# Block 1's out and down products with tokens on the partitions, seven products for eight in two pairs of k-tiles

## The chip, the cores and the metric

The kernel runs on one core of one Trainium2 chip. The metric is the device time of one execution in microseconds. Before the change the median of 3 runs is 2539.73 us (2539.48 to 2539.82). One further execution was recorded by the hardware profiler; all durations below come from it.

## The reference

Two transformer blocks on 256 tokens of width 2048, in fp32. The change lies in the end of the first block (`w_out` is 2048 x 2048, `w_gate` and `w_up` are 2048 x 5632, `w_down` is 5632 x 2048):

```python
    h = h + mixed @ w_out                                        # "out"
    hn = rmsnorm(h, ffn_norm)
    h = h + (silu(hn @ w_gate) * (hn @ w_up)) @ w_down           # "gu", then "down"
return rmsnorm(h, final_norm)                                    # input of block 2
```

Block 2 begins with another rmsnorm and a large input projection, of which the values `dv` are taken first.

## The kernel before, in words

Precision. TensorE multiplies in a rounded fp32 format, so every operand is split into a high and a low part and a product takes three matmuls: high by high, high by low, low by high. Weights arrive from HBM in pieces `raw` of 128 x 1024 (512 KB, one DMA on SyncE's queue, 6 buffers). ScalarE copies a piece into `wh`, VectorE subtracts into `wl` (`halves`, L391 to L398). `wh` and `wl` have 4 buffers each, and a fifth from the pool `wx1` while out, gu and down run. So a piece can be split only when TensorE has finished the piece four or five places earlier. Activations are split the same way by `hl` (L418 to L422). A k-tile is 128 rows of a weight.

Two forms of a product. In the form of `mm_w` (L434, L435) the weight is the stationary operand and all 256 tokens stream: a matmul of 512 columns (high weight by both halves of the input) and one of 256 columns. The result has output columns on the partitions, its two halves are added by `sum_halves` (L572 on ScalarE, L575 on VectorE). Out (L434, 8 groups of 2 output tiles) and down are done so. In the form of `group_t` (L525) 128 tokens are stationary and 512 weight columns stream: three matmuls of 512 columns per product, tokens on the partitions. gu is done so: 11 groups, each with 512 columns of gate and 512 of up, 16 pieces (one k-tile each), 4 products per piece. The result goes through Silu (L1030) and a multiply (L1031) to the tile `z`, and TensorE turns it back by 8 transposes per group (L1042), which `hl` splits for down.

Order. Part p of the FFN is 4, 4 and 3 groups of gu, then down over those 16, 16 and 12 k-tiles, added to h (L1068). In the last part each finished tile of h is split for block 2 (`hl` with `gfp`), squared twice on ScalarE (`sq`, 2 buffers) and the squares are summed on GpSimd (`ssq`, L605); the two norms follow (L613, L623). The program is written as Python in program order with small tasks (`pump`, `tick`) set between matmuls; the framework below it places the instructions of each engine in one list, and an engine works through its list in order. `group_t` has code for pairs of k-tiles, which `PAIRS = 0` switches off.

Of the kernel before, what the change touches and what calls it, by code (L numbers as in the profile page):

```python
# [28 lines left out]
PARTS_T = ((0, 16), (16, 16), (32, 12))  # L29
UCOLS = 2048  # L30
PAIRS = 0
# [18 lines left out]
def weight_plan():  # L50
# [50 lines left out]
    for g in range(8):  # L101
        group(("out", g), "w_out", range(16), [(256 * g, 256 * g + 256)])
    for p, (i0, n) in enumerate(PARTS_T):
        for g in range(i0 // 4, (i0 + n) // 4):
            cr = [(512 * g, 512 * g + 512)]
            for c in range(PAIRS // 2):
                ka, kb = [2 * c, 2 * c + 1], [PAIRS + 2 * c, PAIRS + 2 * c + 1]
                unit(("gup", g, c, 0), ("w_gate", ka, cr), ("w_up", kb, cr))
                unit(("gup", g, c, 1), ("w_up", ka, cr), ("w_gate", kb, cr))
            for k in range(2 * PAIRS, KD, 2):  # L110
                unit(("guk", g, k), ("w_gate", [k], cr), ("w_up", [k], cr), ("w_gate", [k + 1], cr), ("w_up", [k + 1], cr))
        chunks = _chunks(range(i0, i0 + n))
        for g, c in [(0, 0), (1, 0), (0, 1), (1, 1)] + [(g, c) for g in range(2, 8) for c in range(2)]:
            unit(("down", p, g, c), ("w_down", chunks[c], [(256 * g, 256 * g + 256)]))
# [24 lines left out]
def _width(ranges):  # L139
# [10 lines left out]
FIRST_OPS = ("B11", "t3", "t1", "B22", "B21", "t2", "t4")  # L150
OPS2 = (("B11", 0), ("B11", 1), ("t3", 0), ("t3", 1), ("t1", 0), ("t1", 1), ("B22", 0), ("B21", 0),
        ("t2", 0), ("t2", 1), ("B22", 1), ("B21", 1), ("t4", 0), ("t4", 1))
assert PAIRS in (0, 4)


def stream():

    out, u = [], 0
    while u < len(PLAN):
        key, n = PLAN[u][0], UNIT_COLS[u]  # L160
        if key[0] == "lat":
# [81 lines left out]

class Prog:
# [5 lines left out]
    def __init__(self, tc, t, dbg=None, stop=None):  # L250
# [7 lines left out]
        self.look, self.far, self.held = 2, 4, {}  # L258
# [75 lines left out]
    def take(self):  # L334

        self.fill(1)
        return self.split.pop(0)

    def fill(self, n=None):
        while len(self.split) < (n or self.look):  # L340
            if not self.raws and not self.fetch():
                return
            while len(self.raws) <= self.far and self.fetch():
                pass
            self.divide()

# [3 lines left out]
    def fetch(self):  # L350
# [3 lines left out]
        nc, w = self.nc, self.t["w"]  # L354
        p = STREAM[self.nraw]
        self.nraw += 1
        if len(p) == 3:
            u, a, b = p
            raw = self.raw(b - a)
            nc.sync.dma_start(raw[:, :b - a], w[u][:, a:b])  # L360
        else:
            op, u = p
            if op == "B11":
                raw = self.wx.tile([P, 1024], F32, tag="sum", name="sum", bufs=4)
                nc.sync.dma_start(raw, w[u][:, 0:1024])
                self.held[u] = raw
            elif op in ("t1", "t2", "t4"):
                raw = self.held[u]
            else:
                raw = self.raw(1024)  # L370
                v, a = {"B22": (u, 1024), "B21": (u + 1, 1024), "t3": (u + 1, 0)}[op]
                nc.sync.dma_start(raw, w[v][:, a:a + 1024])
                if op == "t3":
                    nc.gpsimd.dma_start(raw, w[u][:, 1024:2048], accum_op=ALU.add)
# [3 lines left out]
    def divide(self):  # L378

        nc, w = self.nc, self.t["w"]  # L380
        p, raw = self.raws.pop(0)
        n = p[2] - p[1] if len(p) == 3 else 1024
        self.split.append((p, *self.halves(raw, n)))
        if len(p) == 2:
            u = p[1]
            add = {"B11": (u + 1, 0), "t1": (u, 1024), "t2": (u + 1, 1024)}.get(p[0])
            if add:
                nc.gpsimd.dma_start(raw, w[add[0]][:, add[1]:add[1] + 1024], accum_op=ALU.add)

    def halves(self, raw, n):  # L390
        nc = self.nc  # L391
# [4 lines left out]
        nc.scalar.activation(wh[:, :n], raw[:, :n], AF.Copy)  # L396
        nc.vector.tensor_tensor(wl[:, :n], raw[:, :n], wh[:, :n].bitcast(F32), op=ALU.subtract)  # L397
# [66 lines left out]

# [28 lines left out]
    def combos(self, xa, xb):  # L493
# [5 lines left out]
        nc.vector.tensor_tensor(f[:, 0, :], a2, b2, op=ALU.subtract)  # L499
        nc.vector.tensor_tensor(f[:, 1, :], a1, f[:, 0, :], op=ALU.subtract)  # L500
        nc.vector.tensor_tensor(f[:, 2, :], b1, f[:, 1, :], op=ALU.subtract)
        nc.vector.tensor_tensor(f[:, 3, :], a1, a2, op=ALU.subtract)
        o = self.ffp.tile([P, 2, 4, P], F32R, tag="combo", name="combo", bufs=PAIRS)
# [4 lines left out]
    def group_t(self, xs, cs, before_std=None):  # L508
# [4 lines left out]
        self.one = 7  # L513
        nstd = KD - 2 * PAIRS
        banks = [self.psp.tile([P, 512], F32, tag=f"bank{i}", name="q", bufs=1) for i in range(7)]
        std = [[0, 1], [2, 3]] if not PAIRS else [[1, 2], [3, 7]]
        left = [3 * PAIRS] * 7 + [0]
        for r in std:
            for i in r:
                left[i] += 3 * nstd  # L520
        begun = [False] * 8

        def mm(i, x, w):
            left[i] -= 1
            nc.tensor.matmul(banks[i], x, w, start=not begun[i], stop=left[i] == 0)  # L525
            begun[i] = True
            self.tick(229)

        def product(i, x, w):
            mm(i, x[0], w[0])  # L530
            mm(i, x[0], w[1])
            mm(i, x[1], w[0])
# [3 lines left out]
        for _ in range(7 * (PAIRS // 2)):  # L536
            (op, u), wh, wl = self.take()
            self.fill()
            c = PLAN[u][0][2]
            for i in range(2):  # L540
                a = 2 * c + i
                b = a + PAIRS
                w = [h[:, 512 * i:512 * i + 512] for h in (wh, wl)]
# [1005 lines left out]
```

## Time and profile before

| what | value |
|---|---|
| median of 3 runs | 2539.73 us |
| profiled execution, its own time | 2539.54 us |
| its span in the profile | 2537.7 us |
| TensorE busy | 2507.2 us, 99% of the span |
| VectorE busy | 1633.6 us, 64% |
| ScalarE busy | 1313.2 us, 52% |
| GpSimd busy | 129.7 us, 5% |
| out | 523 to 612 us |
| gu and down, part 1 | 612 to 792, 792 to 883 us |
| gu and down, part 2 | 883 to 1061, 1061 to 1152 us |
| gu and down, part 3 | 1152 to 1286, 1286 to 1354 us |
| first group of dv (block 2) | 1354 us to about 1370 us |

The time lies 1.8 us above the span: what is before the first and after the last recorded instruction. Matmuls are pipelined, so the rows of a busy TensorE overlap; what one costs is the distance between two starts.

### The profile page before, as it was taken

What the parts mean: (1) busy time and instruction counts of PE and PEld (TensorE: products, weight loads), DVE (VectorE), ACT (ScalarE), POOL (GpSimd) and SP (SyncE); (2) the same over time, 40 slices, a digit from 0 to 9 for tenths busy, and PEclk for the clock granted to TensorE, in tenths of its full rate; (3) what the DMA queues carried; (4) which work ended last, traced back from release to release, by engine and by line L of the source; (5) the groups of instructions that cost most, each with busy time, mean ns of one, the idle gap of its engine ahead of it and who ended that gap; (6) DMA issues with size and microseconds to landing.
All of it is one profiled execution on the core that took longest, in us unless ns stands there. A gap on an engine that the chain in (4) does not pass through costs nothing.

```text
span 2537.7 us, 35945 instructions
## 1 busy us (share of the span) xinstructions
PE 2507.2 (99%) x13756; PEld 2168.1 (85%) x13756; DVE 1633.6 (64%) x2379; ACT 1313.2 (52%) x1983; POOL 129.7 (5%) x149
## 2 busy tenths in 40 slices
PE   9999999999999999999999999999999999999997
PEld 8988888888888888888889888888888888888886
DVE  8866775876455544555467677666876567656765
ACT  6565565554444444444456555555655455545553
POOL 3000000001000000000022000003100000000002
PEclk9999999999999999999999999999999999999998
DMA  6544555565555555555555544454555555555552
GB/s 235 201 156 142 172 176 187 188 214 202 184 187 187 189 189 187 189 185 190 187 174 179 193 156 153 143 202 153 171 186 183 191 191 187 182 192 188 190 175 92
DMA packets 131725, 458.52 MB, mean 181 GB/s; under 512 B 14624, under 2 KB 17056, under 8 KB 131296
## 3 DMA queue, kind: packets, MB, share of 16 engines
q1 hardware_dynamic: 130608, 452.78, 52.9%
q10 hardware_dynamic: 944, 3.43, 0.4%
q8 instruction: 108, 1.77, 0.3%
q14 instruction: 65, 0.53, 0.1%
HBM read 454.06 MB, written 2.10 MB: 180 GB/s over the span
## 4 chain that ended last, share of the span: by engine, by line
PE 96%; DVE 3%; ACT 1%; issue 0%; DMA 0%; POOL 0%; POOLq 0%; SPq 0%; ACTq 0%; DVEq 0%
PE acc L434 42%; PE acc L435 21%; PE q L525 19%; PE acc L432 3%; PE acc L480 2%; PE acc L479 2%; PE acc L481 2%; PE acc L431 2%; PE ms L685 1%; PE ms L1209 1%; DVE hl L422 1%; PE ms L714 1%; PE tr L1042 0%; DVE wl L397 0%; PE acc L1340 0%
## 5 line engine op out<-in xcount | busy, mean ns | idle before, releaser
L434 PE MATMUL acc<-hl,wh 128*128 128x512 f32 x4642 | 1646.0, 397 | 7.7 <-DVE hl L422 6.3
L397 DVE TENSOR_TENSOR wl<-raw,wh 128x1024 fp32r<-128x1024 f32 (+4 forms) x882 | 1052.5, 1196 | 704.5 <-ACT wh L396 700.6
L396 ACT ACTIVATE wh<-raw 128x1024 fp32r<-128x1024 f32 (+4 forms) x882 | 907.3, 1031 | 774.9 <-PE acc L434 428.7
L435 PE MATMUL acc<-hl,wl 128*128 128x256 f32 x4642 | 1300.0, 281 | 0.6 <-DVE wl L397 0.5
L434 PEld LDWEIGHTS acc<-hl,wh 128*128 128x128 f32 x4642 | 872.1, 188 | 207.9 <-DVE hl L422 5.7
L435 PEld LDWEIGHTS acc<-hl,wl 128*128 128x128 f32 x4642 | 876.5, 189 | 10.4 <-DVE wl L397 1.9
L525 PE MATMUL q<-wh,hl 128*128 128x512 f32 x1408 | 438.8, 392 | 0.4 <-ACT z L1030 0.4
L525 PEld LDWEIGHTS q<-wh,hl 128*128 128x128 f32 x1408 | 263.0, 188 | 56.2 <-ACT z L1030 0.9
L525 PE MATMUL q<-wl,hl 128*128 128x512 f32 x704 | 275.6, 392 | 0.0
L572 ACT ACTIVATE ev<-acc 128x256 f32<-128x256 f32 x352 | 129.3, 384 | 216.8 <-PE acc L432 215.3
L605 POOL TENSOR_TENSOR ssq<-ssq,sq 128x256 f32<-128x256 f32 x92 | 87.6, 961 | 2058.7 <-ACT sq L595 1585.3
L575 DVE TENSOR_TENSOR tmp<-acc,ev 128x256 f32<-128x256 f32 x321 | 126.5, 422 | 76.5 <-ACT ev L572 76.3
L525 PEld LDWEIGHTS q<-wl,hl 128*128 128x128 f32 x704 | 132.3, 188 | 28.7
L432 PE MATMUL acc<-hl,wh 128*128 128x512 f32 x352 | 132.0, 395 | 0.0
L431 PE MATMUL acc<-hl,wl 128*128 128x256 f32 x352 | 100.8, 286 | 0.0
L480 PE MATMUL acc<-wl,hl 128*128 128x512 f32 (+4 forms) x264 | 90.6, 343 | 2.4 <-DVE wl L397 2.4
L479 PE MATMUL acc<-wh,hl 128*128 128x512 f32 (+4 forms) x264 | 92.4, 350 | 0.0
L481 PE MATMUL acc<-wh,hl 128*128 128x512 f32 (+4 forms) x264 | 90.4, 343 | 0.0
L431 PEld LDWEIGHTS acc<-hl,wl 128*128 128x128 f32 x352 | 66.1, 188 | 8.3 <-issue 0.3
L432 PEld LDWEIGHTS acc<-hl,wh 128*128 128x128 f32 x352 | 66.4, 189 | 7.5
L480 PEld LDWEIGHTS acc<-wl,hl 128*128 128x128 f32 x264 | 49.8, 189 | 5.8 <-DVE wl L397 3.0
L481 PEld LDWEIGHTS acc<-wh,hl 128*128 128x128 f32 x264 | 49.7, 188 | 3.0
(243 smaller groups left out, 1238.9 us busy)
## 6 DMA issues: line engine op xcount, KB each, us to landing
raw<-in_w_dram SPq DMA_DIRECT2D x801, 512.0 KB, 3.6
raw<-in_w_dram SPq DMA_DIRECT2D x18, 384.0 KB, 3.2
raw<-in_w_dram SPq DMA_DIRECT2D x16, 362.0 KB, 4.1
raw<-in_w_dram SPq DMA_DIRECT2D x16, 346.0 KB, 3.6
raw<-in_w_dram SPq DMA_DIRECT2D x15, 256.0 KB, 3.2
raw<-in_w_dram SPq DMA_DIRECT2D x8, 364.0 KB, 3.7
raw<-in_w_dram SPq DMA_DIRECT2D x8, 348.0 KB, 3.6
x<-in_xT_dram SPq DMA_DIRECT2D x8, 256.0 KB, 5.7
```

What stands on the lines that cost most here:

```text
L396: nc.scalar.activation(wh[:, :n], raw[:, :n], AF.Copy)
L397: nc.vector.tensor_tensor(wl[:, :n], raw[:, :n], wh[:, :n].bitcast(F32), op=ALU.subtract)
L431: nc.tensor.matmul(acc[:, S:], wl, x[:, 0, :], start=False, stop=False)
L432: nc.tensor.matmul(acc, wh, x, start=False, stop=True)
L434: nc.tensor.matmul(acc, wh, x, start=first, stop=False)
L435: nc.tensor.matmul(acc[:, S:], wl, x[:, 0, :], start=False, stop=last)
L479: nc.tensor.matmul(acc, xh, wh, start=(k == 0), stop=False)
L480: nc.tensor.matmul(acc, xh, wl, start=False, stop=False)
L481: nc.tensor.matmul(acc, xl, wh, start=False, stop=(k == n - 1))
L525: nc.tensor.matmul(banks[i], x, w, start=not begun[i], stop=left[i] == 0)
L572: nc.scalar.activation(e, acc[:, S:], AF.Copy)
L575: nc.vector.tensor_tensor(out, acc[:, :S], e, op=ALU.add)
```

## The change

Out and down now use the form of `group_t`: 2 groups of 1024 output columns each, for out over 16 k-tiles, for down over 16, 16 and 12. h lies with tokens on the partitions (`h0`, `h1`, loaded from a second copy of x, `xtok`), and what the next stage needs is turned by `turned`: after out 32 transposes, after the last down 32.

In every group of out, gu and down four k-tiles form two pairs. For a pair the 2 x 2 block product (two halves of the tokens, two k-tiles, two blocks of 512 columns) is computed by seven products (`OPS`) in place of eight, after Winograd. The activation side of it, four differences per pair, is made once by `combos`. The weight side, four sums per pair (`t1`, `t3`, `t2`, `t4`), is made anew in every group by VectorE, in place in the raw pieces (L431, 128 x 1024 for both pairs at a time), and each sum is split like a piece. So the four pieces of the two pairs give seven pieces for TensorE (6 matmuls each) and the other k-tiles give one each (12 matmuls). Four of the seven results are combined at the end of the pair part (`sums`, "early", L616 to L620), four accumulators hold the rest until the end of the group ("late", L1156 in gu, L636 in out and down). In out and down both are added to h (L632, L636).

Banks, look-ahead and raw buffers are kept by hand (`map`, `look`, `ahead`, `live`); the pool `wx1` is gone, so `wh` and `wl` have four buffers. Tiles of h for block 2 are turned two at a time (`done`): per tile `hl`, two squares with their GpSimd sums, and a copy of h. The transposes of the second half stand in the first group of `dv`.

```diff
+OUT_PAIRS = ((0, 1), (2, 3))
+GU_PAIRS = ((0, 4), (1, 5))
+DOWN_PAIRS = ((0, 1), (2, 3))
...
-PAIRS = 0
...
+    def tgroup(key, w, kts, pairs, col):
+        kts = list(kts)
+        w1, w2 = (w, w) if isinstance(w, str) else w
+        c1 = [(col, col + 512)]
+        c2 = [(col + 512, col + 1024)] if isinstance(w, str) else c1
+        for c in range(0, len(pairs), 2):
+            pp = pairs[c:c + 2]
+            ka, kb = [kts[a] for a, _ in pp], [kts[b] for _, b in pp]
+            seg = lambda w, kk, c: [(w, [k], c) for k in kk]
+            unit(key + ("pair", c, 0), *seg(w1, ka, c1), *seg(w2, kb, c2))
+            unit(key + ("pair", c, 1), *seg(w2, ka, c2), *seg(w1, kb, c1))
+        rest = [k for i, k in enumerate(kts) if not any(i in p for p in pairs)]
+        for i in range(0, len(rest), 2):
+            unit(key + ("std", i), *[x for k in rest[i:i + 2] for x in ((w1, [k], c1), (w2, [k], c2))])
...
-    for g in range(8):
-        group(("out", g), "w_out", range(16), [(256 * g, 256 * g + 256)])
+    for g in range(2):
+        tgroup(("out", g), "w_out", range(16), OUT_PAIRS, 1024 * g)
...
-            unit(("down", p, g, c), ("w_down", chunks[c], [(256 * g, 256 * g + 256)]))
+            tgroup(("gu", g), ("w_gate", "w_up"), range(16), GU_PAIRS, 512 * g)
+        for g in range(2):
+            tgroup(("down", p, g), "w_down", range(i0, i0 + n), DOWN_PAIRS, 1024 * g)
...
+OPS = ("B11", "B22", "t1", "t3", "t2", "B21", "t4")
+ROLES = {"B11": 0, "B22": 1, "t1": 2, "t3": 3, "t2": 4, "B21": 5, "t4": 6, "std": 7}
+EARLY, LATE = (0, 2, 3, 4), (1, 5, 6, 7)
...
+            if op == "t1":
+                parts["B12"] = get(u + 1, 0, n)
+            elif op in ("B11", "B22"):
+                parts[op] = get(u, 0 if op == "B11" else n, n if op == "B11" else 2 * n)
+            elif op == "B21":
+                parts[op] = get(u + 1, n, 2 * n)
...
+            to, a, b = {"B11": ("B11", 0, 0), "B22": ("B22", 0, 0), "B21": ("B21", 0, 0), "t1": ("B11", "B11", "B12"),
+                        "t3": ("B12", "B12", "B22"), "t2": ("B11", "B11", "B22"), "t4": ("B11", "B11", "B21")}[op]
+            raw = parts[to]
+            if op == "t2":
+                self.live -= 1
+            if a:
+                self.nc.vector.tensor_tensor(raw[:, :n], parts[a][:, :n], parts[b][:, :n], op=ALU.add)
...
+        def product(r, x, w):
+            if r not in b:
+                b[r] = place(r)
+            for i, j in ((0, 0), (0, 1), (1, 0)):
+                nc.tensor.matmul(b[r], x[i], w[j], start=left[r] == total[r], stop=left[r] == 1)
+                left[r] -= 1
+                self.tick(229)
...
+            for op in OPS:
+                p, wh, wl = self.take()
+                self.fill()
+                for i, (ka, kb) in enumerate(pairs[c:c + 2]):
+                    w = [h[:, 512 * i:512 * i + 512] for h in (wh, wl)]
+                    cmb = lambda m: (cs[c + i][:, 0, m, :], cs[c + i][:, 1, m, :])
+                    x = {"B11": lambda: cut(xs[ka], t0), "B21": lambda: cut(xs[kb], t0), "B22": lambda: cmb(2),
+                         "t4": lambda: cut(xs[kb], t1), "t1": lambda: cmb(0), "t2": lambda: cmb(1),
+                         "t3": lambda: cmb(3)}[op]()
+                    product(op, x, w)
...
+        if pairs:
+            early(b)
...
+        late(b)
+        self.map = [self.map[i] for i in EARLY + LATE]
+        self.one = self.map[7]
...
+    def sums(self, b):
+        e, v, w, c = [self.fz.tile([P, 512], F32, tag="ft", name="ft", bufs=4) for _ in range(4)]
+        nc.scalar.activation(e, b["B11"], AF.Copy)
+        nc.vector.tensor_tensor(v, b["t2"], e, op=ALU.subtract)
+        nc.vector.tensor_tensor(w, b["t1"], v, op=ALU.add)
+        nc.vector.scalar_tensor_tensor(c, b["t3"], -1.0, w, op0=ALU.mult, op1=ALU.add)
+        nc.vector.tensor_tensor(v, b["t3"], v, op=ALU.subtract)
+        return e, w, v, c
+    LATE_OF = ("B21", "B22", "t4", "std")
+    def residual(self, h, g):
+        at = [h[t][:, 1024 * g + 512 * m:1024 * g + 512 * m + 512] for t in range(2) for m in range(2)]
+        def early(b):
+            for a, x in zip(at, self.sums(b)):
+                nc.vector.tensor_tensor(a, a, x, op=ALU.add)
+        def late(b):
+            for a, r in zip(at, self.LATE_OF):
+                nc.vector.tensor_tensor(a, b[r], a, op=ALU.add)
...
+    def turned(self, src, n, done, wait):
+        for i in range(0, n, 2):
+            b = self.bank("tr")
+            for j in range(2):
+                for t in range(2):
+                    o = 256 * j + 128 * t
+                    self.nc.tensor.transpose(b[:, o:o + P], src[t][:, (i + j) * P:(i + j + 1) * P], self.cst("ident"))
+            for j in range(2):
+                done(i + j, b[:, 256 * j:256 * j + 256])
+            yield
...
+            for a, b in OUT_PAIRS:
+                if j == b:
+                    cm.append(self.combos(gates[a][0], za, self.cbp))
...
+            early, late = self.residual(h, g)
+            self.group_t(("out", g), mixed, cm, OUT_PAIRS, early, late)
...
+                def late(b):
+                    for i, r in enumerate(self.LATE_OF):
+                        if sb_:
+                            nc.vector.tensor_tensor(sb_[i], b[r], sb_[i], op=ALU.add)
+                        else:
+                            sb_.append(b[r])
+                self.group_t(("gu", g), hn, cs, GU_PAIRS, early, late)
...
+                early, late = self.residual(h, g)
+                operands = Acts(acts, n)
+                self.group_t(("down", p, g), operands, ca, DOWN_PAIRS, early, late,
+                             lambda k: k >= need and self.finish(t0))
+                if last:
+                    src = [h[t][:, 1024 * g:1024 * g + 1024] for t in range(2)]
+                    def done(i, s, g=g):
+                        nonlocal sa, sb
+                        j = 8 * g + i
+                        x2.append(self.hl(s, self.gfp[:, j:j + 1]))
+                        sa = self.stat_add(sa, s)
+                        sb = self.stat_add(sb, s, self.col("final_norm", j))
+                        r = self.resp.tile([P, S], F32, tag="res", name="res", bufs=16)
+                        nc.scalar.activation(r, s, AF.Copy)
+                        hs.append(r)
+                    t0 = self.add(self.turned(src, 8, done, 3), urgent=True)
...
+            accs = self.group_a(lambda c: (c == 2 and self.finish(tx), self.load("dv", g, c))[1], x, 4, n)
...
-                self.wx = c2.enter_context(tc.tile_pool(name="wx1", bufs=1))
-                self.wxn = 1
```

On VectorE, at the seam from one gu group to the next, this stands in the list before (wl: the split of a piece, L397; z: the multiply with up; hl: the split of a turned tile):

```order
L397 TENSOR_TENSOR wl<-raw,wh 128x1024 x14
L1031 SCALAR_TENSOR_TENSOR z<-q,small,z 128x512 x2
L397 TENSOR_TENSOR wl<-raw,wh 128x1024
L419 TENSOR_TENSOR hl<-tr,hl 128x256 x2
L397 TENSOR_TENSOR wl<-raw,wh 128x1024
L419 TENSOR_TENSOR hl<-tr,hl 128x256 x2
```

A group has 16 splits of pieces, two multiplies and four small splits, and no sum of weights. At the same seam the list is now (L453: split; L431: sum of two raw pieces; L1156: late sum; L1129: z; L479: hl; L617: first of the early sums):

```order
L431 TENSOR_TENSOR raw<-raw 128x1024 x2
L453 TENSOR_TENSOR wl<-raw,wh 128x1024
L1156 TENSOR_TENSOR ft<-q,ft 128x512
L453 TENSOR_TENSOR wl<-raw,wh 128x1024
L1156 TENSOR_TENSOR ft<-q,ft 128x512 x3
L1129 SCALAR_TENSOR_TENSOR z<-ft,small,z 128x512 x2
L431 TENSOR_TENSOR raw<-raw 128x1024
L453 TENSOR_TENSOR wl<-raw,wh 128x1024 x3
L431 TENSOR_TENSOR raw<-raw 128x1024
L479 TENSOR_TENSOR hl<-tr,hl 128x256
L617 TENSOR_TENSOR ft<-q,ft 128x512
L453 TENSOR_TENSOR wl<-raw,wh 128x1024
```

In front of the first row stands the split of B11; the splits after it are B22, t1, then t3, t2, B21, and last t4. Four sums of 1024 columns, four late sums and the two multiplies have come between the seven splits.

On ScalarE, at the entry to block 2, the list before (hl: high part of an input tile of block 2; sq: a square, which waits for GpSimd to free one of its two buffers; wh: a piece's high part; ev: half of an accumulator):

```order
L396 ACTIVATE wh<-raw 128x692 x2
L572 ACTIVATE ev<-acc 128x256 x2
L396 ACTIVATE wh<-raw 128x692
L421 ACTIVATE hl<-res,gfp 128x256
L595 ACTIVATE sq<-res 128x256
L595 ACTIVATE sq<-res,cc 128x256
L421 ACTIVATE hl<-res,gfp 128x256
L595 ACTIVATE sq<-res 128x256
L595 ACTIVATE sq<-res,cc 128x256
L396 ACTIVATE wh<-raw 128x692 x2
```

Two tiles are left to be squared there when dv begins. Now the eight rows behind the first of the following stand there four times, for the eight tiles of the second half, each time after the transposes of two tiles:

```order
L449 ACTIVATE wh<-raw 128x692
L481 ACTIVATE hl<-tr,gfp 128x256
L680 ACTIVATE sq<-tr 128x256
L680 ACTIVATE sq<-tr,cc 128x256
L1181 ACTIVATE res<-tr 128x256
L481 ACTIVATE hl<-tr,gfp 128x256
L680 ACTIVATE sq<-tr 128x256
L680 ACTIVATE sq<-tr,cc 128x256
L1181 ACTIVATE res<-tr 128x256
```

The second `hl` of a block stands behind the first tile's squares and copy, and all four pairs of tiles go through one bank of PSUM.

## Rows read from the trace of the kernel before

**Rows 1.** The page's chain that ended last, shares of the span by engine.
```profile
PE 96%; DVE 3%; ACT 1%; issue 0%; DMA 0%; POOL 0%; POOLq 0%; SPq 0%; ACTq 0%; DVEq 0%
```

**Rows 2.** Stretches, busy PE PEld DVE ACT POOL us (instructions), clock, DMA share, GB/s.
```profile
523.00:612.00 89.00, 89.00 (x510) 77.68 (x509) 62.57 (x79) 49.03 (x77) 11.65 (x13) 1.00 0.64 219
657.00:792.00 135.00, 134.65 (x599) 109.90 (x600) 67.52 (x67) 59.33 (x68) 0.00 (x0) 1.00 0.55 187
792.00:883.00 91.00, 91.00 (x524) 79.66 (x524) 51.86 (x68) 40.41 (x53) 0.00 (x0) 1.00 0.55 186
1286.00:1354.00 68.00, 68.00 (x391) 59.35 (x390) 50.99 (x72) 44.86 (x84) 23.71 (x27) 1.00 0.48 161
1354.00:1372.00 18.00, 18.00 (x119) 17.79 (x119) 13.97 (x31) 11.58 (x22) 4.64 (x6) 1.00 0.54 179
```

**Rows 3.** TensorE in order of time, end of out: start us, us, instruction.
```profile
610.00 0.39 PE L434 MATMUL acc<-hl,wh 128*128 128x512 f32 x1
610.24 0.28 PE L435 MATMUL acc<-hl,wl 128*128 128x256 f32 x1
610.35 0.39 PE L434 MATMUL acc<-hl,wh 128*128 128x512 f32 x1
```

**Rows 4.** TensorE in order of time, in gu.
```profile
745.46 0.39 PE L525 MATMUL q<-wl,hl 128*128 128x512 f32 x1
...
746.14 0.39 PE L525 MATMUL q<-wl,hl 128*128 128x512 f32 x1
```

**Rows 5.** TensorE in order of time, four transposes between the matmuls of gu.
```profile
661.60 0.61 PE L1042 MATMUL tr<-cc,z 128*128 128x128 f32 x4
661.97 0.47 PE L525 MATMUL q<-wl,hl 128*128 128x512 f32 x1
662.29 0.63 PE L525 MATMUL q<-wh,hl 128*128 128x512 f32 x2
```

**Rows 6.** VectorE in order of time in gu; in brackets the idle time before and its releaser.
```profile
1239.42 1.23 DVE L397 TENSOR_TENSOR wl<-raw,wh 128x1024 fp32r<-128x1024 f32 x1 [1.49 <-ACT wh L396]
1240.56 1.40 DVE L1031 SCALAR_TENSOR_TENSOR z<-q,small,z 128x512 f32<-128x512 f32 x2
```

**Rows 7.** Groups on VectorE and ScalarE: busy us, mean ns of one, idle before, releaser.
```profile
L397 DVE TENSOR_TENSOR wl<-raw,wh 128x1024 fp32r<-128x1024 f32 x801 | 981.0, 1227 | 668.2 <-ACT wh L396 664.7 <-PE acc L1340 2.0
L575 DVE TENSOR_TENSOR tmp<-acc,ev 128x256 f32<-128x256 f32 x321 | 126.5, 422 | 76.5 <-ACT ev L572 76.3
L419 DVE TENSOR_TENSOR hl<-tr,hl 128x256 fp32r<-128x256 f32 x44 | 18.4, 421 | 10.9 <-ACT hl L418 10.9
L1031 DVE SCALAR_TENSOR_TENSOR z<-q,small,z 128x512 f32<-128x512 f32 x22 | 15.5, 744 | 1.0 <-ACT z L1030 0.8 <-issue 0.2
L396 ACT ACTIVATE wh<-raw 128x1024 fp32r<-128x1024 f32 x801 | 845.5, 1057 | 717.2 <-PE acc L434 397.4 <-PE q L525 251.7 <-issue 29.9
```

**Rows 8.** Waits on ScalarE, 657 to 792 us: total, times, longest.
```profile
ACT wh L396 <- PE q L525: 66.4, 43, 1.8
```

**Rows 9.** GpSimd in order of time, at the entry to block 2.
```profile
1356.97 3.25 POOL L605 TENSOR_TENSOR ssq<-ssq,sq 128x256 f32<-128x256 f32 x4 [3.45 <-ACT sq L595]
1363.75 0.70 POOL L623 TENSOR_TENSOR small<-small,mhalf 128x2 f32<-128x2 f32 x1 [3.52 <-DVE small L628]
```

**Rows 10.** Stretches around two stalls of TensorE in block 2, as rows 2.
```profile
1764.50:1766.70 2.20, 0.00 (x0) 0.00 (x1) 2.20 (x4) 1.55 (x5) 1.99 (x3) 0.98 0.65 257
1766.70:1769.90 3.20, 3.17 (x10) 2.72 (x11) 3.20 (x4) 1.02 (x2) 3.20 (x5) 0.50 0.00 0
1773.30:1776.20 2.90, 0.42 (x3) 0.10 (x1) 2.90 (x5) 1.88 (x5) 2.90 (x4) 1.00 0.00 0
1776.20:1780.10 3.90, 3.88 (x14) 3.23 (x15) 3.90 (x8) 2.79 (x7) 2.15 (x3) 0.58 0.00 0
```

**Rows 11.** Waits on TensorE over the whole span, gu's: total, times, longest.
```profile
PE q L525 <- ACT z L1030: 0.4, 1, 0.4
```

**Rows 12.** The page's DMA issues: KB each, median us from issue to landing.
```profile
raw<-in_w_dram SPq DMA_DIRECT2D x801, 512.0 KB, 3.6
```

More of the change, by code (lines that the diff above doesn't have):

```diff
@@ L378, in divide, with low_due, high @@
     def divide(self):
-        nc, w = self.nc, self.t["w"]
         p, raw = self.raws.pop(0)
[L382 to L391, printed above, removed]
+        if isinstance(p[0], int):
+            n = p[2] - p[1]
+        else:
+            op, u, n = p
+            parts = self.parts[u]
+            to, a, b = {"B11": ("B11", 0, 0), "B22": ("B22", 0, 0), "B21": ("B21", 0, 0), "t1": ("B11", "B11", "B12"),
[5 more added lines that the diff above has]
+                self.nc.vector.tensor_tensor(raw[:, :n], parts[a][:, :n], parts[b][:, :n], op=ALU.add)
+        wh, wl = self.high(raw, n)
+        self.low_due()
+        self.due = (wl, raw, wh, n, p[0])
+        self.split.append((p, wh, wl))
+    def low_due(self):
+        if self.due:
+            self.low(*self.due[:4])
+            if self.due[4] not in ("B11", "t1", "t2", "B22"):
+                self.live -= 1
+            self.due = None
+    def high(self, raw, n):
         self.nhalf += 1
@@ L506, in combos, with group_t @@
         return o
-    def group_t(self, xs, cs, before_std=None):
+    def group_t(self, key, xs, cs, pairs, early, late, extra=None):
         nc = self.nc
[L513 to L532, printed above, removed]
+        n = len(xs)
+        paired = {k for p in pairs for k in p}
+        rest = [k for k in range(n) if k not in paired]
+        b = {}
+        place = lambda r: self.psp.tile([P, 512], F32, tag=f"bank{self.map[ROLES[r]]}", name="q", bufs=1)
+        self.one = self.map[7]
+        left = dict.fromkeys(OPS, 3 * len(pairs))
+        std = (("B21", "B22"), ("t4", "std"))
+        left["std"] = 0
+        for r in std[0] + std[1]:
+            left[r] += 3 * len(rest)
+        total = dict(left)
+        def product(r, x, w):
[5 more added lines that the diff above has]
+                self.tick(229)
@@ L534, in group_t @@
         t0, t1 = slice(0, P), slice(P, S)
         cut = lambda x, ts: (x[:, 0, ts], x[:, 1, ts])
[L536 to L543, printed above, removed]
-                cmb = lambda n: (cs[a][:, 0, n, :], cs[a][:, 1, n, :])
-                q, x = {"B11": (0, cut(xs[a], t0)), "B21": (1, cut(xs[b], t0)), "B22": (2, cmb(2)),
-                        "t4": (3, cut(xs[b], t1)), "t1": (4, cmb(0)), "t2": (5, cmb(1)), "t3": (6, cmb(3))}[op]
-                product(q, x, w)
@@ L1073, in block1_ffn @@
+        self.look, self.ahead = 2, False
+        self.fill()
+        self.one, self.trb = None, (self.nbank + 7) % 8
         n1, n12 = Norm(), Norm()
         def factors():
+            while not t0.done:
+                yield
             yield
```

297 lines of the change are left out of this document (139 added, 158 removed).

## The prediction

> **What bounds the kernel now.** I read the chain of waits first: 96% of it is TensorE, and DMA has nothing [rows 1]. [...] Three gu groups take 135.0 us, so one takes 45.0. Then the distances between matmul starts, since busy rows overlap. In the form of out and down one k-tile by 128 output columns takes 0.35 us (610.00 to 610.35) [rows 3]; two of them do the work of one product of gu, which takes 0.68 us (745.46 to 746.14), 0.227 per matmul [rows 4]. Last, what VectorE and ScalarE wait for: the split of a weight piece waits for its high part, and that waits for TensorE to free a buffer [rows 6, 7, 8]. So the splitters run on a leash of four or five pieces. On the average they have time to spare, but they cannot work ahead of the leash.
>
> The sum is made against the profiled execution, 2539.5 us, which lies 0.2 us under the median of the runs.
>
> **What TensorE saves.** Seven for eight: 2 pairs in each of 2 + 11 + 6 = 19 groups, 38 products by 0.68 = 25.8 us less. The other form: out and down are 16 x 8 + 44 x 8 = 480 products, each 2 x 0.35 - 0.68 = 0.02 us cheaper, 9.6 us less. Against it stand 64 more transposes. Four of them and one matmul take 661.60 to 662.29, 0.69 us [rows 5]; without the matmul's 0.227 that is 0.115 each, 7.4 us more. Alone, these would make 28.0 us less. That the products are really gone is not in doubt: the lists show the seven names and no eighth.
>
> The halves of the accumulators that ScalarE and VectorE added in out and down go (each 0.42 us on VectorE) [rows 7]. Neither engine is on the chain there, so I give nothing for it.
>
> **What the pair part costs.** TensorE's side first, with its zero where it starts on B11: six matmuls per piece, so 1.36 us each; it wants B22 at 1.36, t1 at 2.72, t3 at 4.08, t2 at 5.44, B21 at 6.8, t4 at 8.16, and the first ordinary piece at 9.53. An ordinary piece lasts 2.72. With four buffers a split can begin when the piece four places earlier is done: B11 at -8.16, B22 at -5.44, t1 at -2.72, t3 at 0.
>
> VectorE's side. A split takes 1.23 us, but the next instruction starts after 1.14 (1239.42 to 1240.56) [rows 6]. No row shows a sum of two 1024-column fp32 pieces; the split is the same operation on the same shape, so I take 1.14 for it too; bounds are 0.42 (the row of a quarter of the size) and 1.23 [rows 7]. For a late sum or the first early sum (512 columns, from PSUM) no row stands either; between 0.42 (half the size) and 0.74 (the z multiply) I take 0.61: the row of half the size and 0.28 more (a quarter of the split's 1.14 for a quarter of its columns), less the 0.09 by which the next one starts early. By the same 0.09 or so a multiply z is 0.66 and a small split 0.34 [rows 7]. From the first split of the pair part to the first ordinary one, a gu group that follows a gu group gives VectorE 8 splits and 4 sums (13.7 us), 4 late sums (2.4), 2 multiplies (1.3), 2 small splits (0.7), one early sum (0.6): 18.7 us. It can begin at -6.85 (-8.16, the drain of the last matmul, 1.06 for the high part [rows 7]) and would end at 11.9 without a pause. TensorE wants that last split at 9.75, or 10.55 with its eight transposes counted in, which I do above and in the old 45.0 us.
>
> In the order of the list: B11 to -5.7; two sums to -3.4; split of B22 to -2.3; a pause for the first late sum, whose accumulator TensorE ends at -1.9, to -1.2; split of t1 to -0.1; three late sums, each after its last matmul, to 1.75; two multiplies to 3.1; sum t2 to 4.2; split of t3 to 5.35, wanted at 4.3. The high part of t2 follows its sum, to 5.4, and TensorE's list has a matmul with it ahead of the rest of t3, so TensorE pauses about 0.8 there. Splits of t2 and B21 to 7.7; sum t4 to 8.9; its high part, ScalarE, to 10.1, while VectorE does a small split and the early sum; split of t4 to 11.2; small split; first ordinary split to 12.7. TensorE has paused for t4 from 9.3 to 10.1 and from 10.3 to 11.4, and gets the first ordinary piece going at about 13.2 with the transposes done. That is 2.6 us late. Behind it the ordinary pieces need 2.72 us of TensorE and 1.14 of VectorE each, and VectorE is back at its leash within three of them.
>
> This holds for 8 gu groups and for the 3 first halves of down (which follow a gu group). The other 8 pair parts (both of out, the gu groups behind out or down, the second halves of down) have no multiplies and mostly no small splits before t4: the same count gives t4's split at 9.9 to 10.4 and 1.7 to 2.2 us late, more in the second half of out, where small splits stand ahead of t4; I take 2.1. Sum: 11 x 2.6 + 8 x 2.1 = 45.4 us. Bounds: below, the queue without any pause, 11 x 1.3 + 0 = 14; above, with full durations (20 instructions by 0.09 more), 11 x 4.3 + 8 x 3.7 = 77.
>
> **The entry to block 2.** Before, two tiles were left when dv began, and TensorE stood still nowhere in 1354 to 1372 [rows 2]. Now eight tiles are turned there through one bank, two at a time. ScalarE may square only when GpSimd has freed a buffer, and GpSimd takes 0.81 us per sum (four in 3.25) [rows 9], so 1.6 per tile. With the high part, the copy and a weight piece in between a round of two tiles takes 3.3 to 4.1 us. In it TensorE has 12 dv matmuls of 346 columns (346/512 of 0.227 = 0.153 each), its transposes and in two rounds six matmuls of the next group: 2.3 to 3.2 us. Four rounds lose 4 to 6 us, and the norm behind them (matmul, 0.70 on GpSimd [rows 9], matmul) loses about 2, since GpSimd's last sums end later than the tiles. I take 7; bounds 0 (all hidden by moving matmuls forward) and 13.
>
> **The sum.** 2539.5 - 25.8 - 9.6 + 7.4 + 45.4 + 7 = 2563.9 us, in a measurement 2564. With the bounds of the unknown prices 2526 (14 and 0) to 2602 (77 and 13).
>
> **Rivals.** A: the pair parts are hidden. Against it stands the queue above; for it, that VectorE is idle 30 to 50% of these stages [rows 2] and that pauses between groups were 0.4 us at most [rows 11]. With 0.4 per pair part, 7.6 us, and the entry at 7, the time is 2526, with a free entry 2519. The change gains as long as a pair part loses less than (28.0 - 7)/19 = 1.1 us.
>
> [...]
>
> C, slow too: raw pieces late. The sums are made in place, so the raw buffer of B11 is free only after t4's split at 11.2; the piece loaded into it lands 3.6 us later [rows 12], is split by 17.5 and wanted at 18.6. If landings take 5 us when four are issued together, each group loses about 1 us more, 19 us, 2583.
>
> D: no overlap between VectorE's instructions, and 77 us for the pair parts: 2539.5 - 28.0 + 77 + 7 = 2595. The rows speak against it (1.14 from start to start, 1.23 of duration) [rows 6]. [...]
>
> **Chances and range.** Forecast (pair parts of 1.3 to 4 us) 0.55, A 0.25, B 0.10, C 0.06, D 0.04. The forecast's own range is 2545 to 2585. The range for 8 in 10 takes A in down to 2518 and B, D up to 2596. What a measurement of this kernel tells from no change is about 0.2%, 5 us: faster (under 2534.7) holds A and nothing else, 0.25; within it a little of A and of the forecast's low end, 0.08; slower 0.67.
>
> **What would show it.** In the changed kernel's profile TensorE should wait in every pair part, for the split or the high part of t3, t2 and t4 (L453, L449), 2 to 3 us in a gu group, and a gu group should take 45.5 to 46.5 us, where A has 43.5. Out should take 88 to 91 us, down of 16 k-tiles 89 to 92. VectorE should show no idle time from -6 to 13 us around a pair part. At the entry TensorE should wait for ScalarE's hl behind GpSimd's sums. I am wrong if the waits at t4 are under 1 us, if VectorE's sums turn out much shorter than a split, or if the granted clock falls in gu.

## The result and the profile after

The changed kernel takes 2558.91 us (median of 4 runs, 2558.57 to 2559.29) against 2539.78 of the kernel before in the same session: 1.0076 times as long, 95% interval 1.0058 to 1.0093. The forecast was 2564, slower, range 2518 to 2596. The profiled span is 2557.5 us; 19.8 us were added.

The chain of waits that ended last in the changed kernel, from its page, stands against [rows 1]: VectorE now has a tenth of it, and the weight sums (L431) and splits (L453) stand on it by name.

```profile
PE 85%; DVE 10%; issue 2%; ACT 2%; DMA 0%; POOL 0%; POOLq 0%; ACTq 0%; SPq 0%; DVEq 0%
PE acc L494 33%; PE q L578 23%; PE acc L495 17%; DVE wl L453 4%; PE acc L492 2%; PE acc L527 2%; PE acc L526 2%; PE acc L528 1%; DVE raw L431 1%; PE acc L491 1%; ACT wh L449 1%; PE ms L770 1%; DVE ft L1156 1%; DVE hl L482 1%; PE ms L1326 1%
```

The changed kernel by stage, columns as in [rows 2]: out, four gu groups, a down of 16 k-tiles, the next four gu groups, the last three, and the entry to block 2 with its dv products.

```profile
522.30:612.40 90.10, 88.07 (x389) 71.00 (x388) 75.27 (x93) 49.88 (x66) 0.00 (x0) 1.00 0.61 210
612.40:794.30 181.90, 177.22 (x786) 143.22 (x785) 142.59 (x166) 97.19 (x120) 0.69 (x1) 1.00 0.56 185
794.30:884.60 90.30, 87.45 (x381) 70.26 (x380) 71.14 (x77) 42.21 (x45) 0.00 (x0) 1.00 0.55 187
884.60:1065.20 180.60, 175.18 (x770) 141.71 (x769) 138.82 (x154) 91.04 (x105) 0.00 (x0) 1.00 0.55 187
1155.50:1290.40 134.90, 130.76 (x575) 106.17 (x574) 104.25 (x116) 68.41 (x79) 0.00 (x0) 1.00 0.56 187
1361.80:1423.20 61.40, 55.06 (x324) 50.58 (x324) 34.99 (x64) 34.86 (x67) 14.40 (x20) 0.97 0.48 164
```

The eleven gu groups take 181.9 + 180.6 + 134.9 = 497.4 us, 45.2 each on the mean. In the kernel before, three of them took 45.0 each [rows 2] and all eleven 44.8 on the mean (from the first gu product to the first of down: 611.74 to 792.29, 882.64 to 1061.51 and 1152.10 to 1285.97 us). TensorE has 1.36 us less to do in a group (two products by 0.68) and yet needs longer. VectorE is busy 78% of the time in gu. The clock is 1.00 in all lines but the last.

Where the 19.8 us lie is read from the starts of the first dv product and of the first product behind that stage, in the lists of TensorE in order of time. Kernel before:

```profile
1354.42 0.33 PE L479 MATMUL acc<-wh,hl 128*128 128x346 f32 x1
1402.22 0.39 PE L434 MATMUL acc<-hl,wh 128*128 128x512 f32 x1
```

Changed kernel:

```profile
1361.86 0.32 PE L526 MATMUL acc<-wh,hl 128*128 128x346 f32 x1
1423.19 0.39 PE L494 MATMUL acc<-hl,wh 128*128 128x512 f32 x1
```

So 7.4 us are lost until dv begins, 13.5 in the dv stage (61.3 for 47.8), and 1.1 come back later; why stays open.

Now one pair part, that of a gu group that follows a gu group, VectorE in order of time (start, duration, what ended the idle time before it; "..." stands for rows left out). TensorE's zero is the start of its first product of B11, 1.37 before its first product with a combination of activations, which starts at 750.06: 748.69.

```profile
741.84 1.23 DVE L453 TENSOR_TENSOR wl<-raw,wh 128x1024 fp32r<-128x1024 f32 x1 [1.49 <-ACT wh L449]
743.10 2.49 DVE L431 TENSOR_TENSOR raw<-raw 128x1024 f32<-128x1024 f32 x2
...
747.47 1.22 DVE L453 TENSOR_TENSOR wl<-raw,wh 128x1024 fp32r<-128x1024 f32 x1
...
750.40 1.41 DVE L1129 SCALAR_TENSOR_TENSOR z<-ft,small,z 128x512 f32<-128x512 f32 x2
751.72 1.22 DVE L431 TENSOR_TENSOR raw<-raw 128x1024 f32<-128x1024 f32 x1
752.86 3.57 DVE L453 TENSOR_TENSOR wl<-raw,wh 128x1024 fp32r<-128x1024 f32 x3
756.34 1.22 DVE L431 TENSOR_TENSOR raw<-raw 128x1024 f32<-128x1024 f32 x1
...
758.68 1.22 DVE L453 TENSOR_TENSOR wl<-raw,wh 128x1024 fp32r<-128x1024 f32 x1 [0.19 <-ACT wh L449]
```

A sum takes 1.22 and the next instruction starts 1.14 later (751.72 to 752.86), as the prediction took it. In this pair part the queue runs to a tenth of a microsecond as it was counted: B11's split from -6.85, t1's done at 0.0, the multiplies at 3.1, t3's, t2's and B21's splits at 7.7, t4's sum at 8.9, t4's split at 11.2. TensorE in the same stretch:

```profile
753.04 0.60 PE L649 MATMUL tr<-cc,z 128*128 128x128 f32 x4
754.09 0.50 PE L578 MATMUL q<-wh,combo 128*128 128x512 f32 x1 [0.44 <-ACT wh L449]
...
757.87 0.39 PE L578 MATMUL q<-wh,hl 128*128 128x512 f32 x1
758.70 0.50 PE L578 MATMUL q<-wh,hl 128*128 128x512 f32 x1 [0.44 <-ACT wh L449]
759.92 0.50 PE L578 MATMUL q<-wh,hl 128*128 128x512 f32 x1 [0.72 <-ACT wh L449]
```

From start to start it loses 0.6 in front of t2's product (1.05 for four transposes, which need 0.46), 0.6 in front of t4's (0.83 for 0.227) and 1.0 behind its first matmul (1.22 for 0.227); with 0.3 for the matmuls that start slowly after a stop (754.09 and 759.92 have 0.34 to the next start for 0.227), 2.5 us. The bracket alone shows less, because the modelled end of a matmul (0.39 from its start) lies behind the start of the next (0.227). Counted so, the 19 pair parts lose 38.5 us: about 2.4 in each of the 11 that follow a gu group, about 1.5 in each of the 8 others.

### The profile page after: what moved, and what is told of

It reads as the page before. It is cut to its first block, busy times and chain, and to the rows that moved or that the text cites. A ratio compares the mean times of both kernels' runs of the same rounds, so it can differ in the third digit from the quotient of the medians.

```text
span 2557.5 us, 35199 instructions
## 1 busy us (share of the span) xinstructions
PE 2495.7 (98%) x13218; PEld 2129.2 (83%) x13218; DVE 1841.6 (72%) x2617; ACT 1366.4 (53%) x2036; POOL 119.3 (5%) x134
## 4 chain that ended last, share of the span: by engine, by line
PE 85%; DVE 10%; issue 2%; ACT 2%; DMA 0%; POOL 0%; POOLq 0%; ACTq 0%; SPq 0%; DVEq 0%
PE acc L494 33%; PE q L578 23%; PE acc L495 17%; DVE wl L453 4%; PE acc L492 2%; PE acc L527 2%; PE acc L526 2%; PE acc L528 1%; DVE raw L431 1%; PE acc L491 1%; ACT wh L449 1%; PE ms L770 1%; DVE ft L1156 1%; DVE hl L482 1%; PE ms L1326 1%
## 5 line engine op out<-in xcount | busy, mean ns | idle before, releaser
L453 DVE TENSOR_TENSOR wl<-raw,wh 128x1024 fp32r<-128x1024 f32 (+4 forms) x939 | 1116.0, 1198 | 536.4 <-ACT wh L449 532.8
L494 PE MATMUL acc<-hl,wh 128*128 128x512 f32 x3746 | 1327.3, 397 | 7.4 <-DVE hl L482 6.5
L495 PE MATMUL acc<-hl,wl 128*128 128x256 f32 x3746 | 1049.0, 281 | 0.7 <-DVE wl L453 0.7
L494 PEld LDWEIGHTS acc<-hl,wh 128*128 128x128 f32 x3746 | 703.5, 188 | 166.9 <-DVE hl L482 6.0
L495 PEld LDWEIGHTS acc<-hl,wl 128*128 128x128 f32 x3746 | 708.2, 189 | 9.2 <-DVE wl L453 2.0
L578 PE MATMUL q<-wh,hl 128*128 128x512 f32 x1988 | 628.4, 392 | 18.5 <-ACT wh L449 17.9
L578 PEld LDWEIGHTS q<-wh,hl 128*128 128x128 f32 x1988 | 372.0, 188 | 107.5 <-ACT wh L449 30.8
L578 PE MATMUL q<-wl,hl 128*128 128x512 f32 x994 | 388.6, 391 | 0.9 <-DVE wl L453 0.8
L492 PE MATMUL acc<-hl,wh 128*128 128x512 f32 x288 | 108.3, 396 | 0.0
L578 PE MATMUL q<-wh,combo 128*128 128x512 f32 x304 | 100.8, 396 | 4.2 <-ACT wh L449 4.2
L431 DVE TENSOR_TENSOR raw<-raw 128x1024 f32<-128x1024 f32 x76 | 92.8, 1221 | 1.3
L491 PE MATMUL acc<-hl,wl 128*128 128x256 f32 x288 | 82.9, 288 | 0.0
```

The lines of the kernel that those rows point to most:

```text
L431: self.nc.vector.tensor_tensor(raw[:, :n], parts[a][:, :n], parts[b][:, :n], op=ALU.add)
L453: self.nc.vector.tensor_tensor(wl[:, :n], raw[:, :n], wh[:, :n].bitcast(F32), op=ALU.subtract)
L491: nc.tensor.matmul(acc[:, S:], wl, x[:, 0, :], start=False, stop=False)
L492: nc.tensor.matmul(acc, wh, x, start=False, stop=True)
L494: nc.tensor.matmul(acc, wh, x, start=first, stop=False)
L495: nc.tensor.matmul(acc[:, S:], wl, x[:, 0, :], start=False, stop=last)
```

## The experiments

The theory (Q): VectorE's queue in a pair part is longer than what four wh/wl buffers let it begin early, and TensorE waits for its end. Rivals: the hand-overs between the engines are slow whatever VectorE has to do (H), the products with combinations are dear in themselves (T).

**1. Without the weight sums.**

```
-            if a:
+            if a and False:
                 self.nc.vector.tensor_tensor(raw[:, :n], ..., op=ALU.add)
```

> The changed kernel without the four sums of weight pieces per pair part (76 in all), so the products t1 to t4 use unsummed weights. Theory Q (VectorE's queue in the pair part is too long for what the four wh/wl buffers let it begin early): the queue gets 4 x 1.14 = 4.6 us shorter, the waits for t2 and t4 go, the 38 us that TensorE stands in the pair parts fall under 8, and the time is 2523 to 2532 us, forecast 2526. Rival H (hand-overs: each piece goes through ScalarE, VectorE and TensorE in turn, and the pieces are late by that, whatever VectorE has to do): no more than a third of it goes, 2545 to 2559. Rival T (products with combined activations are dearer on TensorE itself): no change, 2557 to 2561.

Measured 2520.00 us, 38.9 less than the changed kernel and 3.0 below Q's window; ratio to before 0.9923 (0.9910 to 0.9935). What TensorE waited for most from out up to dv in the changed kernel (total, times, longest):

```profile
PE q L578 <- ACT wh L449: 22.1, 43, 0.8
```

Without the sums, up to 1335 us, these two and a third of 0.2 are all. The second line belongs to dv, which begins at 1322.3 here.

```profile
PE q L578 <- DVE wl L453: 0.5, 1, 0.5
PE acc L526 <- ACT hl L481: 1.7, 2, 0.9
```

The 38.9 are as much as the whole loss of the pair parts, six more than the 2526 forecast here had it. H and T are out: same hand-overs, same combinations, and hardly a wait.

**2. A fifth pair of wh and wl buffers.** The change had dropped it.

```
+                    self.wx = c2.enter_context(tc.tile_pool(name="wx1", bufs=1))
+                    self.wxn = 1
...
+        self.wx = None
         self.fill()
```

> The changed kernel with a fifth pair of wh and wl buffers in block 1's out, gu and down, as the kernel before had; nothing else. The scheduler then also puts the sum of t2 ahead of the late sums. Theory Q: the queue of a pair part can begin 2.7 us earlier, which is as much as it is late now; the loss per pair part falls from 2.0 to under 0.5, and the time is 2523 to 2532, forecast 2526, like without the sums. Rival C (the loads are then late, since the sums in place hold up to four of six raw buffers): TensorE's waits move to the weight pieces' DMA and half of the gain is lost, 2538 to 2548. Rival H (hand-overs): under 5 us of gain, 2554 to 2559.

Measured 2532.54 us (ratio 0.9972, 0.9961 to 0.9983): 26.4 less than the changed kernel, and 7.2 less than the kernel before. VectorE in the same group, whose zero is now 743.76:

```profile
734.12 1.23 DVE L453 TENSOR_TENSOR wl<-raw,wh 128x1024 fp32r<-128x1024 f32 x1 [1.57 <-ACT wh L449]
735.38 2.48 DVE L431 TENSOR_TENSOR raw<-raw 128x1024 f32<-128x1024 f32 x2
...
740.89 1.22 DVE L431 TENSOR_TENSOR raw<-raw 128x1024 f32<-128x1024 f32 x1
...
749.15 1.23 DVE L431 TENSOR_TENSOR raw<-raw 128x1024 f32<-128x1024 f32 x1
...
752.30 2.35 DVE L453 TENSOR_TENSOR wl<-raw,wh 128x1024 fp32r<-128x1024 f32 x2
```

B11's split begins at -9.6 instead of -6.85, t2's sum ends at -1.6 instead of 4.2, t4's sum at 6.6 instead of 8.9 and its split at 9.7 instead of 11.2. This group loses 0.2 us, all 19 together 5.7 instead of 38.5, as forecast. The time missed its window by half a microsecond all the same; experiment 8 shows the larger part of why. C (late loads) is out as a rule: TensorE waits for no load. Once, in the last of the 19 parts, a sum of VectorE waited for one:

```profile
1292.90 1.23 DVE L431 TENSOR_TENSOR raw<-raw 128x1024 f32<-128x1024 f32 x1 [2.17 <-DMA raw<-in_w_dram]
```

**3. One sum per group on GpSimd.**

```
-                self.nc.vector.tensor_tensor(raw[:, :n], ..., op=ALU.add)
+                eng = self.nc.gpsimd if op == "t3" else self.nc.vector
+                eng.tensor_tensor(raw[:, :n], ..., op=ALU.add)
```

> The changed kernel with one of the four weight sums per group (t3's) on GpSimd, which is idle there. Theory Q: VectorE's queue is 1.14 us shorter in each of 19 pair parts, and GpSimd has the sum ready before ScalarE wants it (about 3 us of work from -4.5 on, wanted at 0); 15 to 22 us less, 2537 to 2544. Rival P (GpSimd and VectorE hinder each other on their way to SBUF): VectorE's instructions beside the sum get longer by as much as is saved, 2554 to 2564.

Measured 2578.07 us (ratio 1.0153, 1.0139 to 1.0166): 19 us more than the changed kernel instead of 15 to 22 less. VectorE and GpSimd in order of time:

```profile
745.56 1.23 DVE L454 TENSOR_TENSOR wl<-raw,wh 128x1024 fp32r<-128x1024 f32 x1 [1.49 <-ACT wh L450]
...
748.28 3.46 DVE L454 TENSOR_TENSOR wl<-raw,wh 128x1024 fp32r<-128x1024 f32 x1 [0.23 <-ACT wh L450]
```

```profile
748.27 2.39 POOL L432 TENSOR_TENSOR raw<-raw 128x1024 f32<-128x1024 f32 x1 [44.24 <-ACT wh L450]
```

GpSimd's sum starts 0.01 us ahead of VectorE's split, and the split takes 3.46 instead of 1.23: it stood nearly all of GpSimd's 2.39. So it is in 17 of the 19 pair parts (3.4 to 3.5). In the two others the split started 0.03 us ahead, and GpSimd's sum stood:

```profile
610.43 1.23 DVE L454 TENSOR_TENSOR wl<-raw,wh 128x1024 fp32r<-128x1024 f32 x1 [0.19 <-ACT wh L450]
```

```profile
610.46 3.46 POOL L432 TENSOR_TENSOR raw<-raw 128x1024 f32<-128x1024 f32 x1 [44.52 <-ACT wh L450]
```

In all 19 the one that started first held the other. Where the split stands, VectorE is spared 1.14 and held for 2.2, 1.1 us per pair part worse, about the 19 us that were measured. Rival P, in a stronger form than written: P had VectorE's instructions longer by the 1.14 that is saved, the split is longer by 2.2, and in the two other parts the sum by 1.1 (3.46 for 2.39). Where the two meet, which P puts on their way to SBUF, no run shows.

**4. No pairs.** OUT_PAIRS, GU_PAIRS and DOWN_PAIRS are empty, and a group takes the other four banks for its accumulators; out and down stay in the new form.

> The changed kernel without pairs of k-tiles (eight products again, no sums of weights or activations), all else as changed: out and down with tokens on the partitions, four buffers, the entry to block 2. Theory Q: 38 products by 0.68 come back (+25.8), TensorE's loss in the pair parts goes (-38.5, less some 0.3 of ordinary pause per group, +6): 2548 to 2556, forecast 2552. It stays above the time of the kernel before by what the entry to block 2 loses (about 12 us), less 2 us that the form gives. If the loss is not in the pair parts but in the form or in the buffers (rival F), the products come back and nothing goes: 2575 to 2587.

Measured 2546.78 us (ratio 1.0028, 1.0017 to 1.0039), 1.2 under the window. F is out. The dv products start here:

```profile
1347.34 0.32 PE L526 MATMUL acc<-wh,hl 128*128 128x346 f32 x1
```

That is 7.1 us ahead of the kernel before, what the form is worth up to there, and 14.5 ahead of the changed kernel: its pair parts cost 14.5 + 25.8 = 40.3 us (38.5 where their pauses are counted one by one).

**5. and 6. The entry: copies first, or more buffers of squares.** In the changed kernel a round of two tiles takes 5.3 us (transposes at 1375.17 and 1380.45). ScalarE in one of them:

```profile
1376.21 0.47 ACT L481 ACTIVATE hl<-tr,gfp 128x256 fp32r<-128x256 f32 x1 [0.42 <-PE tr L649]
1377.29 0.38 ACT L680 ACTIVATE sq<-tr 128x256 f32<-128x256 f32 x1 [0.61 <-DVE hl L482]
1377.57 0.47 ACT L680 ACTIVATE sq<-tr,cc 128x256 f32<-128x256 f32 x1
1377.93 0.39 ACT L1181 ACTIVATE res<-tr 128x256 f32<-128x256 f32 x1
1378.19 0.48 ACT L481 ACTIVATE hl<-tr,gfp 128x256 fp32r<-128x256 f32 x1
```

The square waits 0.61 us for VectorE's low part, though both only read the bank; ScalarE is through with a tile after 2.0 us. The profile shows the wait and not its reason; that the two take turns at the bank is theory B's assumption. Two edits:

```
+            if out:
+                at = [out(x) for x in at]
...
-                        nc.scalar.activation(r, s, AF.Copy)
...
+                        nc.vector.tensor_copy(r, x)
```

> The changed kernel, in which the transposed tiles at block 2's entry are first copied out of their bank by VectorE (0.42 us each), and all else (high and low part, both squares) reads the copy. Theory B (one bank and turns at it: ScalarE's squares wait until VectorE has read the bank, the next transposes until ScalarE's copy has read it, 2.0 us per tile): a round of two tiles falls from 5.2 to about 3.6 us, the stage from the first dv product to the first one behind it from 61.3 to 53 to 57 us, and the time is 2550 to 2556, forecast 2553. Theory G (the prediction's: GpSimd's sums at two buffers of squares set the pace): squares wait for GpSimd as before, under 2 us of gain, 2557 to 2560.

```
-        sq = self.tmp("sq", 2)
+        sq = self.tmp("sq", 4)
```

> The changed kernel with four buffers of squares for GpSimd's sums instead of two. Theory G (the prediction's: the squares wait for a buffer that GpSimd frees): 4 us less at the entry, 2553 to 2556. Theory B (turns at one bank): no change, 2558 to 2560.

Measured 2558.10 us with the copies (ratio 1.0072, 1.0059 to 1.0085) and 2560.18 with four buffers (1.0081, 1.0067 to 1.0095). More buffers give nothing (1.3 us more), and the squares still wait for VectorE there, 5.2 us in five waits, so GpSimd was not what the entry waited for. The copies give 2.6 us in the stage (58.8 for 61.3) and lose 2.2 before it. By its time this run lies in G's window and not in B's, and with the bank out of the way its squares do wait for GpSimd; where G is wrong is "as before", for in the changed kernel they waited for VectorE. ScalarE's and GpSimd's list:

```profile
1375.55 0.51 ACT L683 ACTIVATE sq<-res,cc 128x256 f32<-128x256 f32 x1 [0.46 <-POOL ssq L693]
...
1377.12 0.51 ACT L683 ACTIVATE sq<-res,cc 128x256 f32<-128x256 f32 x1 [0.28 <-POOL ssq L693]
```

```profile
1373.86 6.37 POOL L693 TENSOR_TENSOR ssq<-ssq,sq 128x256 f32<-128x256 f32 x8 [14.65 <-ACT sq L683]
```

Eight sums without a pause, 1.57 us per tile. B was right on the wait and wrong on its worth: two bounds seem to lie one behind the other. The copies together with four buffers of squares, which would test the second, were not run, and the 11.0 us that the stage still takes above the kernel before are not accounted for one by one.

**7. Both remedies.** The fifth buffers, and the copies on VectorE, then on ScalarE (`nc.scalar.activation(r, x, AF.Copy)`).

> The fifth pair of wh and wl buffers and the copies out of the bank together. The two concern different stages, so their gains add: 2532.5 less what the copies alone give (3 to 9, forecast 6), 2523 to 2530, forecast 2526.5. If the entry is paced by what block 1's end leaves behind (rival E), the gain of the copies is smaller here than alone, 2530 to 2533.

> The fifth buffers and the copies out of the bank, the copies now on ScalarE instead of VectorE. With VectorE's copies TensorE stood three times for 0.7 to 1.1 us at the end of block 1 for a split behind them. If these stops come from the copies in VectorE's queue (theory V), they go: 2524 to 2527, forecast 2526. If the round is paced by ScalarE (theory S: it then has 5 operations of 0.3 to 0.45 us per tile), the copies there make it longer and nothing is won: 2528 to 2531.

Measured 2528.73 (ratio 0.9956, 0.9943 to 0.9970) and 2527.93 us (0.9956, 0.9944 to 0.9969). The copies give 3.8 on top of the fifth buffers, where they gave 0.8 alone, and both versions beat the two kernels of the case, the second by 11.8 and 31.0 us. Which engine copies makes no difference that can be told: with ScalarE's copies TensorE still stands twice, 1.8 us in all, for a split at the end of block 1, so V falls.

**8. What a fifth buffer costs.** Without pairs there is no queue to shorten.

> No pairs of k-tiles, and a fifth pair of wh and wl buffers. Theory Q (the fifth buffer pays because the pair parts have more work for VectorE than four buffers let it begin early): without pair parts it gives under 3 us, 2544 to 2548. Rival F (the fifth buffer pays everywhere, at every change of group): 7 us or more, 2535 to 2540.

Measured 2551.72 us (ratio 1.0049, 1.0036 to 1.0061): not less, 4.9 more. TensorE in order of time, the second of the three matmuls of four products; the first two follow one another, and the last two:

```profile
676.73 0.39 PE L578 MATMUL q<-wl,hl 128*128 128x512 f32 x1
677.41 0.39 PE L578 MATMUL q<-wl,hl 128*128 128x512 f32 x1
...
679.48 0.39 PE L578 MATMUL q<-wl,hl 128*128 128x512 f32 x1
680.18 0.39 PE L578 MATMUL q<-wl,hl 128*128 128x512 f32 x1
```

A product takes 0.68 and, in every fifth piece, 0.70. By the count of the pieces that is the one in the fifth buffer: over out, gu and down its matmuls start 233.2 ns apart on the mean, those of the other four 227.0 to 228.5. The kernel before has the same in gu, 233.9 in one piece of five. The mean of all is 228.5 for 227.0 with four buffers; by 3552 matmuls that is 5.4 us. With pairs it is 229.2 for 227.7, 5 of the 33 us (38.5 less 5.7) that experiment 2 should have given. Three runs looked for the reason: the buffer at another place in SBUF with pairs and without (its pool made ahead of `hp`), and its wh and wl in two pools far apart. The first of them changes the second version of experiment 7, which is "the run before" in its text.

> As the run before, with the fifth pair of buffers at another place in SBUF (reserved ahead of h and of the accumulators' copies instead of behind them). In the runs with a fifth buffer the matmuls of every fifth piece start 231 to 236 ns apart instead of 227. Theory A (the place of the buffer): the spacing is 227 everywhere and the time 3 to 6 us less, 2520 to 2523. Theory N (five buffers in turn, wherever they lie): no change against the run before, within 1.5 us.

> No pairs, a fifth pair of buffers at that other place in SBUF. Theory A (place): the 5 us that the fifth buffer cost without pairs go, 2546 to 2548. Theory N (five in turn): 2550 to 2553 as before.

> As the run with the fifth buffers and ScalarE's copies, with the high and the low part of the fifth pair reserved apart in SBUF (h and the accumulators' copies between them), where they were neighbours of 4 KB each; the other four pairs have theirs 16 KB apart. Theory D (the distance of the two parts slows the matmuls that read them in turn): the matmuls of every fifth piece start 227 ns apart like the others, and the time is 3 to 6 us less, 2522 to 2525. Theory N (something else about a fifth buffer): spacing 231 to 236 and the time as before, 2526 to 2530.

Measured 2529.55, 2552.38 and 2529.32 us: no gain, and the same spacing (229.2, 228.6 and 229.4 on the mean of all). Theories A and D fall; why the matmuls of every fifth piece start farther apart stays open.

## Why the prediction came out as it did

The direction, the mechanism of the pair parts and the time were right (2564 for 2558.9), the last with luck: the errors of the single terms add up to 14 us, and it takes their signs to leave 4.6. Term by term, in us:

| term | forecast | measured |
|---|---|---|
| 38 products less | -25.8 | -25.8 (by count) |
| form of out and down, its transposes up to dv | -4.0 | -7.1 |
| pair parts | +45.4 | +40.3 |
| entry, with its 16 transposes (1.8) | +8.8 | +13.5 |
| behind it | 0 | -1.1 |
| sum | +24.4 | +19.8 |

The pair part is the step that carried the prediction, and it held: the queue, instruction by instruction, the two places of the waits (t2, t4), and the price of the sums, which stood in no row. In the 11 dear parts 2.4 was measured for 2.6; in the 8 others 1.5 for 2.1, below the 1.7 to 2.2 of the count; why stays open. A sum of the count is off by a tenth: 9.75 and eight transposes by 0.115 make 10.67, not 10.55. Also, the old 45.0 held what the fifth buffer costs, 192 matmuls at 228.7 ns for 227.0, which is 0.3 us per group and went with that buffer. So a gu group takes 45.2 on the mean, the three that lose less included, where I gave 45.5 to 46.5. Out (90.1) and down (90.3) lie where they were put.

The entry is the step that failed in its mechanism: "ScalarE may square only when GpSimd has freed a buffer". It waited for VectorE's low part (6.8 us in eight waits), and a round took 5.3 us instead of 3.3 to 4.1. The entry without its transposes cost 11.7 us for the 7 that I took; the bound (13) still held it. What ScalarE waited for from 1370 to 1392, and what TensorE waited for most in the stage (total, times, longest):

```profile
ACT sq L680 <- DVE hl L482: 6.8, 8, 1.6
```

```profile
PE acc L526 <- ACT hl L481: 2.3, 4, 0.9
```

And the clock fell there:

```profile
1369.70:1375.80 6.10, 3.96 (x22) 2.81 (x19) 1.76 (x4) 4.22 (x10) 2.66 (x4) 0.96 0.44 159
1375.80:1379.00 3.20, 2.96 (x11) 2.55 (x10) 1.65 (x3) 1.86 (x5) 1.41 (x3) 0.54 0.30 92
```

TensorE stood 2.1 of 6.1 us, never longer than 0.9 at a time, and then ran 3.2 us at a granted clock of 0.54, with dv matmuls of 346 columns 0.28 us apart (1377.19 to 1377.47) that are 0.16 apart at 1.00 (1379.49 to 1379.65). At 1.00 those 3.2 us of work would have taken 1.7 (an estimate, 3.2 x 0.54), so up to 1.5 of the entry's loss is the clock's, for which the entry had no term. The two falls of [rows 10] came behind stops of 2.2 and 2.5 us, and at the very end of the kernel before the clock falls to 0.50 at 2521.0, behind a stop of 1.4 us; which stops bring a fall no run shows. Rival B, TensorE's clock in the pair parts, did not come about: it is 1.00 there throughout, with waits of 0.8 us at most, and no run shows the loss that the range's upper end (2596) takes in for it.

The form gave 3.1 more than I worked out. The kernel before had five buffers in gu, and its matmuls there are 228.7 ns apart for 227.0 in the run without pairs; by 2112 matmuls that is 3.6 us, about what is missing. I had taken 0.68 per product for both.

A is out (the parts are not hidden). C is out: up to dv TensorE waits for no load, and ScalarE for one, 1.9 us. D is out: 1.14 from start to start for the sums too, which last 1.22.

## What to carry to other kernels

When a preparing engine has time on the average but a burst of work at one place, ask how far ahead its buffers let it begin: 38.5 us were lost here with VectorE 78% busy, and one buffer more brought 33 of them back, 26 after what it cost elsewhere. Lay such a queue out against the consumer's clock, instruction by instruction, with start-to-start distances; here it was right to a tenth in the part that was compared. Before work is moved to an idle GpSimd, look what VectorE does at the same time: here a sum of 2.39 us held a split beside it for 2.2 us in 17 of 19 pair parts.

## What the runs showed that was not expected

- GpSimd's sum of two 1024-column pieces (2.39 us) held a VectorE split beside it for 2.2 us: 3.46 instead of 1.23. Where the split started 0.03 us earlier, it was the sum that took 3.46.
- Matmuls that read the fifth of five wh/wl buffers start 233 ns apart, those of the other four 227 to 228.5; another place in SBUF and another distance of wh and wl changed nothing; cause open.
- TensorE's granted clock fell to 0.54 for 3.2 us after several stops of at most 0.9 us, 2.1 of 6.1 us in all; the two falls of [rows 10] in the kernel before came behind stops of 2.2 and 2.5 us.
